# One order for all seven MLP steps, and the last block of the second MLP started on token tiles 0 and 1

## The chip, the cores and the metric

One core of a Trainium2 chip. The metric is the device time of one execution in microseconds (us), the median of several runs. A profile of one further execution shows what each engine did. The engines are TensorE (PE: matrix products; its weight loads are shown as PEld), VectorE (DVE), ScalarE (ACT), GpSimd (POOL) and SyncE (SP, which issues most transfers). Each engine takes the instructions of its own queue in the order in which the program holds them; semaphores make one engine wait for another.

## The reference

Four layers on 512 tokens of width 1024: a mixer with latent attention, an MLP, a mixer with gated linear attention, and a second MLP, each behind an RMS norm and added to the residual; a last RMS norm ends it. The change concerns the MLPs and the last norm alone:

```python
def sq_relu_mlp(xn, w_up, w_down):
    hid = jnp.square(jax.nn.relu(xn @ w_up))
    return hid @ w_down
...
        x = x + sq_relu_mlp(rms_norm(x, norm_mlp[i]), mlp_w_up[i], mlp_w_down[i]).astype(x.dtype)
    return rms_norm(x, final_norm)
```

`w_up` is 1024 x 4096 and `w_down` 4096 x 1024, all in float32.

## The kernel before, in words

**Precision.** A float32 operand is split into two parts of a faster type, high and low (`split`, L122): ACT copies it to the high part (L124), DVE subtracts that from the source to get the low part (L127). A product then takes three matmuls in place of one: high x high, high x low, low x high. `piece` does this for weights (buffers `wh` and `wl`, four of each, used in turn), `parts_of_quad` for a piece of hidden values (four pairs of buffers in turn; a pair with a negative sign is made by L870 and L871). A split writes its buffers only when the matmuls that read their old content are done.

**The MLP** (`mlp`). The 4096 hidden columns are taken in eight blocks of 512. The first block comes from `up_first`. Then seven steps, b = 0 to 6, each compute the hidden values of block b + 1 (up) and add block b's part to the result (down). Both are 2 x 2 block products with seven products instead of eight (Strassen's scheme in Winograd's form): the halves are the two halves of the tokens, of the model width and of the block's columns. The four hidden quads are q11, q12, q21, q22. The seven up-products are named 11, T1, T2, 21, T3, 22 and T4 (24 matmuls of 256 columns each, L993). The seven down-products are d11, d12, d11 + dS1 (here d11'), d12' , S21 (with d22), S5 (with dS1) and the one with dS3: 24 matmuls of 256 columns in the first MLP (MLP 0, L1006), 12 of 512 columns in the second (MLP 1, L1013). The sums of weights are made by transfers of POOL that add to what is in memory (S1, dS1, dS3, half of A2) and by DVE (a11 + S1 and so on).

Results are kept in `S11`, `S12`, `S21`, `SU` and `S5`. Some products go on from what others left in PSUM, so ACT copies a bank or a pair of banks before the next product changes it: product 11 to `y`, T1 to `w2`, and the two-bank sum `d` to `e` (L1021 in the first step, L1130 in the others). `finish` turns an up-product to hidden values: DVE's relu and scale (L885), ACT's square (L886).

PSUM has eight banks here: four single ones, tag "u", and two tiles of two banks each, "d" and "e". A two-bank tile used as two halves is still one tile to the program's tracking of dependencies.

**Two kinds of step.** Step b = 0 is `step` (L1016): up- and down-products alternate, and S5's sum starts fresh in a two-bank tile. Steps 1 to 6 are `step_in_halves` (L1123): seven up-products, then seven down-products. Weights are fetched for the next block as soon as a buffer is free (`after`).

**The last block of MLP 1** (L1270 to L1328). No up-products are left. The four token tiles t of 128 rows by two column halves c are eight row pieces, 12 matmuls of 512 columns each (L1303). A sum is copied into PSUM first by ACT, so the matmuls add to it. For c = 0, the sums of tiles 2, 3 lie in "e" (S12, L1272) and those of 0, 1 in "d" (S11, L1288); for c = 1 each piece has a single bank (L1294). The order is tiles 2, 3, 0, 1. Behind each piece follow the square and its sum along the row (ACT, L1306); for c = 0 a product with the gain (DVE, L1309), for c = 1 the norm's factor (L143, L1315 to L1317), the scaled output of this half (DVE, L1320, reads the PSUM sum) and of the other (ACT, L1322), and their transfers (L1321, L1323).

The order of instructions on each engine is the scheduler's of the framework: it mostly follows the order of the code, and takes an instruction later when its operands or buffers would not be there yet.

Of the kernel before, what the change touches and what calls it, by code (L numbers as in the profile page):

```python
# [15 lines left out]
ALU = mybir.AluOpType  # L16
# [34 lines left out]
def trunk_kernel(ctx: ExitStack, tc: tile.TileContext, t_in: dict, out: bass.AP):  # L51
# [778 lines left out]
    def mlp(layer, nrm, nxt=None):  # L830
# [185 lines left out]
        def step(b, q, r, after):  # L1016
            (q11, q12), (q21, q22) = q

            def begun(src):
                t = two_banks("e")  # L1020
                ACT.activation(t, src, AF.Copy)  # L1021
                return t

            def add(total, t):
                DVE.tensor_tensor(total, laid(t), total, ALU.add)

            def onto(tag, total, a, parts, fresh=False):
                t = two_banks(tag)
                if not fresh:
                    ACT.activation(laid(t), total, AF.Copy)  # L1030
                down_product(t, a, parts, fresh)
                ACT.activation(total, laid(t), AF.Copy)

            A1, A2, s1 = W["A1"], W["A2"], W["S1"]
            a11, a12, s3, a22 = A1[:, :KH], A1[:, KH:], A2[:, :KH], A2[:, KH:]
            d11, d12, ds1, ds3, d22 = (W[n] for n in ("d11", "d12", "dS1", "dS3", "d22"))

            z = bank("u")
            up_product(z, a11, "11", True)
            y = bank("u")  # L1040
            ACT.activation(y, z, AF.Copy)

            d = two_banks("d")
            down_product(d, d11, parts_of_quad(q11), True)
            e = begun(d)

            up_product(y, a12, "21", False)
            finish(y, 0, 0, r)
            DVE.tensor_tensor(a11, s1, a11, ALU.add)

            down_product(e, d12, parts_of_quad(q21), False)
            add(S11, e)
            DVE.tensor_tensor(d11, ds1, d11, ALU.add)
            DVE.tensor_tensor(q12, q22, q12, ALU.subtract)
            DVE.tensor_tensor(q11, q11, q12, ALU.add)

            part = {"e": e}

            def down_11():
                down_product(d, d11, parts_of_quad(q11, -1.0), False)  # L1060
                part["e"] = begun(d)
                DVE.tensor_tensor(d12, d11, d12, ALU.add)
                after("d11")

            def up_t2():
                up_product(z, a11, "T2", False)
                u = part["u"] = tmp()
                ACT.activation(u, z, AF.Copy)
                DVE.tensor_tensor(a12, a11, a12, ALU.add)

            def up_t1():
                w = part["w"] = bank("u")
                up_product(w, s1, "T1", True)
                w2 = part["w2"] = bank("u")
                ACT.activation(w2, w, AF.Copy)  # L1075
                after("S1")

            def down_22():
                e = part["e"]
                down_product(e, d12, parts_of_quad(q22), False)  # L1080
                add(S12, e)
                after("d12")

            def down_12():
                down_product(d, ds3, parts_of_quad(q12), False)
                add(SU, d)
                after("dS3")
                DVE.tensor_tensor(q22, q22, q11, ALU.subtract)

            def up_22():  # L1090
                w = part["w"]
                up_product(w, a12, "22", False)
                c = tmp()
                DVE.tensor_tensor(c, w, part["u"], ALU.add)
                finish(c, 0, 1, r)
                after("A1")

            def up_t3():
                up_product(z, s3, "T3", False)
                v = tmp()  # L1100
                ACT.activation(v, z, AF.Copy)  # L1101
                c = tmp()
                DVE.tensor_tensor(c, part["w2"], v, ALU.add)
                finish(c, 1, 1, r)

            def down_5():
                onto("e", S5, ds1, parts_of_quad(q22, -1.0), True)
                after("dS1")
                DVE.tensor_tensor(q21, q21, q11, ALU.subtract)

            def down_21():
                onto("d", S21, d22, parts_of_quad(q21, -1.0))
                after("d22")

            def up_t4():
                up_product(z, a22, "T4", False)
                finish(z, 1, 0, r)
                after("A2")

            for product in (up_t2, down_11, up_t1, down_22, up_22, up_t3, down_12, up_t4, down_5, down_21):  # L1120
                product()

        def step_in_halves(b, q, r, after):  # L1123
            (q11, q12), (q21, q22) = q
# [8 lines left out]
            def onto(total, a, parts):  # L1133
                pair = [bank("u"), bank("u")]
                cols = [part_of(total, i) for i in range(2)]
                for p, c in zip(pair, cols):
                    copied(laid(p), c)
                down_product(pair, a, parts, False)
                for p, c in zip(pair, cols):
                    copied(c, laid(p))  # L1140
# [45 lines left out]
            onto(S5, ds1, parts_of_quad(q22, -1.0))  # L1186
# [11 lines left out]
        for name in ("S1", "dS1", "d11", "A1", "d12", "dS3", "A2", "d22"):  # L1198
            fetch(0, name)
# [71 lines left out]
        loaded = {1: two_banks("e")}  # L1271
        ACT.activation(loaded[1], S12, AF.Copy)  # L1272
# [8 lines left out]
        rows = {}  # L1281
        for c in range(2):
            for th in (1, 0):
                total = (S11, S12, S21, SU)[2 * c + th]
                if c == 0:
                    if th not in loaded:
                        loaded[th] = two_banks("d")
                        ACT.activation(loaded[th], total, AF.Copy)  # L1288
                    o = loaded[th]
                for i in range(2):  # L1290
                    cs = slice(i * 512, (i + 1) * 512)
                    if c:
                        o = bank("u")
                        ACT.activation(o, total[:, cs], AF.Copy, scale=-1.0)  # L1294
                    rows[2 * th + i, c] = total[:, cs], o if c else o[:, cs]
# [588 lines left out]
```

## Time and profile before

| | |
|---|---|
| median of 3 runs | 1044.69 us (1044.43 to 1044.73) |
| profiled execution | 1042.52 us |
| its span, first to last instruction | 1040.8 us |
| mean granted TensorE clock | 0.999 |
| PE busy | 1030.6 us (99%) |
| DVE busy | 878.5 us (84%) |
| ACT busy | 695.1 us (67%) |
| POOL busy | 113.2 us (11%) |

How to read the lines shown below. The chain of waits goes back from the last instruction to what released each step; its lines give start, length, engine, tile and line, and "x24" the number of instructions. A line of the list of waits gives the waiting engine and line, the one it waited for, the total in us, the number of waits and the longest. A group of instructions shows the line, engine and operation, what is written and read, the shape, the count, then the busy time in us, the mean duration in ns, and the idle time before. A line of the timeline starts with the start and the busy time in us. A line of windows gives the window, its length, the busy time of PE, PEld, DVE, ACT and POOL (with the number of instructions), the granted clock, the share of the DMA engines and GB/s.

### The profile page before, as it was taken

How to read it: one execution, taken by the hardware profiler on the slowest of the kernel's cores; microseconds unless marked ns; L12 is line 12 of the kernel's file. 1: busy time of each engine (PE TensorE's matmuls, PEld its weight loads, DVE VectorE, ACT ScalarE, POOL GpSimd, SP SyncE). 2: the span in 40 equal slices, each digit the busy share in tenths (PEclk: the TensorE clock that was granted, in tenths of full speed). 3: DMA queues.
4: the chain of work that ended last, by engine and by line, in shares of the span. 5: the costliest groups of instructions: out<-in, count | busy, mean ns of one | idle time of the engine just before them, and what ended most of it. 6: DMA issues, size and time to landing. Idle time of an engine off the chain costs nothing.

```text
span 1040.8 us, 16839 instructions
## 1 busy us (share of the span) xinstructions
PE 1030.6 (99%) x6522; PEld 923.2 (89%) x6522; DVE 878.5 (84%) x1343; ACT 695.1 (67%) x1122; POOL 113.2 (11%) x128
## 2 busy tenths in 40 slices
PE   9999999999999999999999999999999999999997
PEld 8788888899999999998888888888889989989985
DVE  7889976899989989989686499469898899898993
ACT  7667754667776876785345565655677677677684
POOL 8400000401101111000000000000011101111000
PEclk9999999999999999999999999999999999999999
DMA  7401214759988778623313212164488777878422
GB/s 234 123 21 41 78 45 148 200 134 223 234 195 204 180 198 203 150 82 122 91 41 95 95 54 82 51 163 148 98 239 203 188 199 191 203 182 198 106 82 82
DMA packets 120001, 145.85 MB, mean 140 GB/s; under 512 B 9488, under 2 KB 86288, under 8 KB 119920
## 3 DMA queue, kind: packets, MB, share of 16 engines
q1 hardware_dynamic: 95424, 113.57, 34.2%
q0 software_dynamic: 22400, 29.36, 17.8%
q10 hardware_dynamic: 2096, 1.84, 0.6%
q8 instruction: 51, 0.84, 0.3%
q14 instruction: 30, 0.25, 0.1%
HBM read 142.39 MB, written 2.10 MB: 139 GB/s over the span
## 4 chain that ended last, share of the span: by engine, by line
PE 92%; DVE 4%; ACT 2%; DMA 1%; issue 1%; SPq 0%; ACTq 0%; DVEq 0%
PE ps L993 25%; PE ps L1006 12%; PE ps L1013 12%; PE ps L132 10%; PE ps L133 10%; PE ps L134 10%; PE ps L1303 2%; PE ps L1264 2%; PE ps L149 1%; PE ps L1523 1%; PE ps L436 1%; PE ps L1650 1%; DVE wl L127 1%; ACT wh L124 1%; DMA comb<-in_mlp_w_down_dram 1%
## 5 line engine op out<-in xcount | busy, mean ns | idle before, releaser
L124 ACT ACTIVATE wh<-wraw 128x1024 fp32r<-128x1024 f32 x139 | 146.3, 1056 | 108.6 <-issue 37.0
L127 DVE TENSOR_TENSOR wl<-wraw,wh 128x1024 fp32r<-128x1024 f32 x139 | 169.5, 1220 | 36.6 <-ACT wh L124 35.8
L993 PE MATMUL ps<-T,wh 128*128 128x256 f32 x896 | 154.8, 275 | 0.1
L127 DVE TENSOR_TENSOR wl<-comb,wh 128x1024 fp32r<-128x1024 f32 x112 | 136.7, 1221 | 16.7 <-ACT wh L124 16.5
L124 ACT ACTIVATE wh<-comb 128x1024 fp32r<-128x1024 f32 x112 | 118.5, 1058 | 47.8 <-issue 28.8
L993 PEld LDWEIGHTS ps<-T,wh 128*128 128x128 f32 x896 | 135.1, 188 | 0.5 <-ACT tmp L1101 0.3
L993 PE MATMUL ps<-T,wl 128*128 128x256 f32 x448 | 123.3, 275 | 0.0
L1013 PE MATMUL ps<-wh,set 128*128 128x512 f32 x392 | 122.8, 390 | 0.2 <-ACT set L124 0.2
L993 PE MATMUL ps<-set,wh 128*128 128x256 f32 x672 | 117.0, 276 | 0.3 <-ACT ps L1075 0.2
L132 PE MATMUL ps<-set,wh 128*128 128x512 f32 x280 | 109.6, 391 | 0.0
L133 PE MATMUL ps<-set,wh 128*128 128x512 f32 x280 | 109.5, 391 | 0.0
L134 PE MATMUL ps<-set,wl 128*128 128x512 f32 x280 | 109.2, 390 | 0.0
L1006 PE MATMUL ps<-hidden_parts,wh 128*128 128x256 f32 x784 | 106.6, 275 | 0.0
L993 PEld LDWEIGHTS ps<-set,wh 128*128 128x128 f32 x672 | 101.9, 188 | 1.4 <-ACT ps L1075 0.4
L1006 PEld LDWEIGHTS ps<-hidden_parts,wh 128*128 128x128 f32 x784 | 97.0, 188 | 0.0
L993 PE MATMUL ps<-set,wl 128*128 128x256 f32 x336 | 92.6, 276 | 0.0
L1013 PEld LDWEIGHTS ps<-wh,set 128*128 128x128 f32 x392 | 73.5, 188 | 15.3 <-ACT set L124 0.4
L993 PEld LDWEIGHTS ps<-T,wl 128*128 128x128 f32 x448 | 84.1, 188 | 0.0
L1013 PE MATMUL ps<-wl,set 128*128 128x512 f32 x196 | 76.3, 389 | 0.0
L993 PEld LDWEIGHTS ps<-set,wl 128*128 128x128 f32 x336 | 63.1, 188 | 0.0
L134 PEld LDWEIGHTS ps<-set,wl 128*128 128x128 f32 x280 | 52.6, 188 | 11.0
L133 PEld LDWEIGHTS ps<-set,wh 128*128 128x128 f32 x280 | 52.6, 188 | 10.9 <-DVE set L765 0.2
(426 smaller groups left out, 2209.8 us busy)
## 6 DMA issues: line engine op xcount, KB each, us to landing
comb<-in_mlp_w_down_dram SPq DMA_DIRECT2D x74, 512.0 KB, 4.4
wraw<-in_mlp_w_up_dram SPq DMA_DIRECT2D x18, 1024.0 KB, 5.6
wraw<-in_mlp_w_up_dram SPq DMA_DIRECT2D x28, 512.0 KB, 5.8
comb<-in_mlp_w_down_dram POOLq DMA_DIRECT2D x28, 512.0 KB, 6.8
wraw<-in_gla_w_in_dram SPq DMA_DIRECT2D x12, 1024.0 KB, 5.2
comb<-in_mlp_w_up_dram SPq DMA_DIRECT2D x14, 512.0 KB, 4.6
comb<-in_mlp_w_up_dram POOLq DMA_DIRECT2D x14, 512.0 KB, 7.3
wraw<-in_mlp_w_up_dram POOLq DMA_DIRECT2D x14, 512.0 KB, 7.6
```

The lines of the kernel that those rows point to most:

```text
L124: order(ACT.activation(hi, src, AF.Copy))
L127: lo_eng.tensor_tensor(lo, src, f(hi), ALU.subtract)
L132: PE.matmul(psum, wh, xh, start=start, stop=False)
L133: PE.matmul(psum, wh, xl, start=False, stop=False)
L134: PE.matmul(psum, wl, xh, start=False, stop=stop)
L149: PE.transpose(psum, src, ident[: src.shape[0], : src.shape[0]])
L436: PE.matmul(p, w[:, i, j * P : (j + 1) * P], x, start=start, stop=stop)
L993: PE.matmul(o, a_, x_, start=start and j == 0 and k == 0 and n == 0, stop=k == KH - 1 and n == 2, skip_group_check=True)
L1006: PE.matmul(o, w_[:, k, j * P : (j + 1) * P], x_[:, ts], start=opens, stop=k == 1 and n == 2, skip_group_check=True)
L1013: PE.matmul(o, x_, w_, start=start and k == 0 and n == 0, stop=k == 1 and n == 2, skip_group_check=True)
L1264: PE.matmul(p, a, x, start=k == 0 and n == 0, stop=k == 3 and n == 2)
L1303: PE.matmul(o, a, b_, start=False, stop=k == 3 and n == 2, skip_group_check=True)
```

## The change

`step` goes, and `step_in_halves` takes its name and is used for every b; in it `onto` gets a flag so that S5's first sum starts fresh. The names of the first fetches are put in another order. In the last block of MLP 1 the sums are seeded by one helper: tiles 0 and 1 in single banks for both column halves, tiles 2 and 3 in the halves of "e" (c = 0) and of "d" (c = 1), and the pieces are computed in the order 0, 1, 2, 3. The hidden quads are split in that order too. The number of matmuls stays the same.

```diff
-            def onto(total, a, parts):
+            def onto(total, a, parts, fresh=False):
                 pair = [bank("u"), bank("u")]
                 cols = [part_of(total, i) for i in range(2)]
-                for p, c in zip(pair, cols):
-                    copied(laid(p), c)
-                down_product(pair, a, parts, False)
+                if not fresh:
+                    for p, c in zip(pair, cols):
+                        copied(laid(p), c)
+                down_product(pair, a, parts, fresh)
...
-            onto(S5, ds1, parts_of_quad(q22, -1.0))
+            onto(S5, ds1, parts_of_quad(q22, -1.0), b == 0)
...
-        for name in ("S1", "dS1", "d11", "A1", "d12", "dS3", "A2", "d22"):
+        for name in ("A1", "S1", "A2", "d11", "dS1", "d22", "d12", "dS3"):
             fetch(0, name)
...
-            (step_in_halves if b else step)(b, Q[b % 2], Q[(b + 1) % 2], after)
+            step(b, Q[b % 2], Q[(b + 1) % 2], after)
...
+        rows = {}
+
+        def seed(o, total, th, c, sign=1.0):
+            for i in range(2):
+                cs = slice(i * 512, (i + 1) * 512)
+                rows[2 * th + i, c] = total[:, cs], o[i]
+                ACT.activation(o[i], total[:, cs], AF.Copy, scale=sign)
+
+        seed([bank("u"), bank("u")], S11, 0, 0)
-        for h, th in ((0, 0), (0, 1), (1, 1), (1, 0)):
+        for h, th in ((0, 0), (0, 1), (1, 0), (1, 1)):
             hid[h, th] = parts_of_quad(q[h][th])
+        seed(split_banks("e"), S12, 1, 0)
...
+        seed([bank("u"), bank("u")], S21, 0, 1, -1.0)
+        seed(split_banks("d"), SU, 1, 1, -1.0)
...
         for c in range(2):
-            for t in (2, 3, 0, 1):
+            for t in range(NT):
                 row(t, c)
```

In the code after the change `step` stands at L1016 to L1087 (its copies to PSUM and from it are L1023), the seeds at L1171, the matmuls of the last block at L1192, and the scaled output of a piece that reads its sum at L1209.

Where the program now holds its instructions, at the three places that matter. In the rows the tile written stands left of the arrow, those read right of it, with their buffer numbers, and in brackets whose semaphores the instruction waits for.

First, ACT's queue in MLP 1's first step. `set_1269` before and `set_1271` after is the first of the four buffers for high parts of hidden quads, and `set_1261` before and `set_1263` after is q11. Before, q11's high part stands among the squares of the first block (L902):

```order
L902 ACTIVATE set_1261_7838<-tmp_1291_7932 128x256 [waits DVE_49]
L902 ACTIVATE set_1262_7839<-tmp_1291_7932 128x256
L124 ACTIVATE wh_1327_8151<-wraw_1314_8086 128x1024 [waits PE_49]
L902 ACTIVATE set_1263_7840<-tmp_1299_7996 128x256 [waits DVE_49]
L902 ACTIVATE set_1264_7841<-tmp_1299_7996 128x256
L124 ACTIVATE set_1269_7846<-set_1261_7838 128x512 [waits Activation_49]
```

After, it stands behind the high part of the weights of d11' (`wh_1361`), whose buffer T4's weights had, and behind the squares of 22 and T4 (L886). The last two rows are a split into the same buffer, which waits for d11's matmuls, and the copy of `d` (`ps2_1350`) to `e` (`ps2_1353`):

```order
L124 ACTIVATE wh_1361_8409<-comb_1316_8092 128x1024 [waits PE_49,Activation_49]
L886 ACTIVATE set_1268_7848<-tmp_1344_8297 128x512 [waits DVE_49]
L886 ACTIVATE set_1269_7849<-tmp_1348_8330 128x512 [waits DVE_49]
L124 ACTIVATE set_1271_7851<-set_1263_7843 128x512
L124 ACTIVATE set_1273_7853<-set_1265_7845 128x512
L124 ACTIVATE set_1271_7851<-set_1266_7846 128x512 [waits DVE_49,PE_49]
L1023 ACTIVATE ps2_1353_8356<-ps2_1350_8337 128x1024 [waits PE_49]
```

The split of q11 has moved from the work of the first block to a place behind the last up-product's finish.

Second, PE's queue at the same place: d12's product on `e`. Before (`e` is `ps2_1326`, `d` is `ps2_1323`) it stands among the matmuls of an up-product:

```order
L993 MATMUL ps_1319_8099<-T_1306_8029,wl_1333_8206 128x256
L993 MATMUL ps_1319_8099<-T_1306_8029,wh_1332_8205 128x256
L1013 MATMUL ps2_1326_8149<-wh_1330_8185,set_1271_7848 128x512 [waits PE_49,Activation_49]
L1013 MATMUL ps2_1326_8149<-wl_1331_8186,set_1271_7848 128x512
L993 MATMUL ps_1319_8099<-T_1306_8029,wh_1332_8205 128x256
```

After, its first three matmuls stand right behind d11's twelve, ahead of S21's (`ps_1354`):

```order
L1013 MATMUL ps2_1350_8337<-wl_1352_8341,set_1271_7851 128x512
L1013 MATMUL ps2_1350_8337<-wh_1351_8340,set_1272_7852 128x512
L1013 MATMUL ps2_1353_8356<-wh_1359_8390,set_1273_7853 128x512 [waits Activation_49]
L1013 MATMUL ps2_1353_8356<-wl_1360_8391,set_1273_7853 128x512
L1013 MATMUL ps2_1353_8356<-wh_1359_8390,set_1274_7854 128x512 [waits DVE_49]
L1013 MATMUL ps_1354_8366<-wh_1356_8370,set_1275_7855 128x512 [waits PE_49,Activation_49]
```

The first matmul on `e` has moved from the middle of an up-product to the place directly behind the product that `e` is a copy of.

Third, PE's queue at the very end: the last two pieces. Before, each has a bank of its own (`ps_1707`, `ps_1708`), and a piece begins when ACT has seeded it:

```order
L1303 MATMUL ps_1707_10900<-set_137,set_1269_7846 128x512 x2
L1303 MATMUL ps_1707_10900<-set_137,set_1270_7847 128x512
L1303 MATMUL ps_1708_10902<-set_137,set_1271_7848 128x512 [waits Activation_49]
L1303 MATMUL ps_1708_10902<-set_137,set_1271_7848 128x512
L1303 MATMUL ps_1708_10902<-set_137,set_1272_7849 128x512
```

After, they are the halves of one tile (`ps2_1712`), and the second one's first matmul waits for DVE:

```order
L1192 MATMUL ps2_1712_10913<-set_137,set_1271_7851 128x512 x2
L1192 MATMUL ps2_1712_10913<-set_137,set_1272_7852 128x512
L1192 MATMUL ps2_1712_10913<-set_137,set_1275_7855 128x512 [waits DVE_49]
L1192 MATMUL ps2_1712_10913<-set_137,set_1275_7855 128x512
L1192 MATMUL ps2_1712_10913<-set_137,set_1276_7856 128x512
```

The wait is for the scaled output of tile 2 (L1209), the only one of DVE's instructions that reads this tile before.

More of the change, by code (lines that the diff above doesn't have):

```diff
@@ L1017, in step @@
             (q11, q12), (q21, q22) = q
[L1019 to L1121, printed above, removed]
@@ L1123, in step_in_halves @@
-        def step_in_halves(b, q, r, after):
-            (q11, q12), (q21, q22) = q
             A1, A2, s1 = W["A1"], W["A2"], W["S1"]
@@ L1270, in mlp @@
         hid = {}
-        loaded = {1: two_banks("e")}
-        ACT.activation(loaded[1], S12, AF.Copy)
-        for h, th in ((0, 0), (0, 1), (1, 1), (1, 0)):
+        rows = {}
[6 more added lines that the diff above has]
+        for h, th in ((0, 0), (0, 1), (1, 0), (1, 1)):
             hid[h, th] = parts_of_quad(q[h][th])
+        seed(split_banks("e"), S12, 1, 0)
         DVE.tensor_tensor(S21, S21, SU, ALU.add)
@@ L1280, in mlp @@
         stats = [sm(3) for _ in range(NT)]
[L1281 to L1295, printed above, removed]
+        seed([bank("u"), bank("u")], S21, 0, 1, -1.0)
+        seed(split_banks("d"), SU, 1, 1, -1.0)
         def row(t, c):
```

## The prediction

> **What bounds the kernel now.** I read the busy times first, then TensorE's waits, then the chain of waits through the three places that the change touches, and last the clock.
>
> ```profile
> PE 1030.6 (99%) x6522; PEld 923.2 (89%) x6522; DVE 878.5 (84%) x1343; ACT 695.1 (67%) x1122; POOL 113.2 (11%) x128
> ```
>
> TensorE (PE) is busy for 1030.6 of 1040.8 us. No other engine can set the time except by making PE wait, and the waits on PE are few:
>
> ```profile
> PE ps L1790 <- DVE ones L195: 1.2, 1, 1.2
> PE ps L1303 <- ACT ps L1272: 1.0, 1, 1.0
> ...
> PE ps L993 <- ACT ps L1075: 0.2, 1, 0.2
> PE ps L1013 <- ACT set L124: 0.2, 1, 0.2
> ```
>
> Three of the four lie where the change works: L1303 is the last block, L993 behind L1075 is the first step of MLP 0, L1013 behind L124 is the first step of MLP 1. Since the count of matmuls doesn't change, the forecast is a sum of PE waits removed and PE waits added. The later steps already have the order that the first one gets, and the chain shows what they cost:
>
> ```profile
> 245.91 19.04 PE ps L993 x168
> 264.95 19.04 PE ps L1006 x168
> ...
> 782.06 19.09 PE ps L993 x168
> 801.14 19.07 PE ps L1013 x84
> ```
>
> A settled step is nothing but PE: 38.08 us in MLP 0 and 38.16 us in MLP 1. From the same rows come the pitches: 19.09/168 = 0.114 us from one 256-column matmul to the next, 19.07/84 = 0.227 us for 512 columns, 2.73 us for one up-product (a seventh of 19.09) and 2.72 us for one down-product.
>
> **MLP 0, first step: a gain.** Before, this step runs from 206.35 to 245.91, and the next one is the settled step:
>
> ```profile
> 206.35:245.91 39.56, 39.16 (x339) 38.56 (x338) 38.97 (x45) 27.44 (x36) 5.34 (x5) 1.00 0.69 179
> 245.91:283.99 38.08, 38.08 (x338) 38.08 (x338) 35.27 (x39) 29.38 (x41) 5.00 (x4) 1.00 0.85 208
> 228.23 0.59 ACT ps L1075
> ...
> 236.90 0.49 ACT tmp L1101
> ```
>
> The first number after the window is its length, the next PE's busy time. The old step is 1.48 us longer than a settled one. Two of the pauses are the chain's detours over ACT's copies (L1075 of T1's bank, L1101 of T3's): the old order follows each copy too soon with a product that needs it. The settled order puts a whole product between a copy and its use, and takes both out. The copy of product 11 (now L1038) is still needed early, by 21, but T1 and T2 now stand between. The hidden quad q11 is split long before its use here, since ACT issues that split among the copies of the first block, as it did before. S1 is now used by the second product instead of the fifth, and POOL, which adds its second quadrant, issued that long ago:
>
> ```profile
> 183.28 1.45 POOL L982 DMA_DIRECT2D comb<-in_mlp_w_up_dram  x1 [103.62 <-DMA comb<-in_mlp_w_up_dram]
> 681.64 1.30 POOL L982 DMA_DIRECT2D comb<-in_mlp_w_up_dram  x1 [184.53 <-PE ps L149]
> ```
>
> That is 20 us and more ahead of the step here, and some 60 ahead in MLP 1. SP's issues keep their order up to the step. In the steps, transfers for the next block are issued in the settled order, in which PE's list has no wait for a DMA: cost nothing, cover over 20 us. I take -1.2 us of the 1.48, with -1.5 if all goes and -0.9 if the pause at the start stays.
>
> **MLP 1, first step: a loss.** Here the order of ACT's rows shows what the chain of before can't. Before, q11's high part was made early, 9 us ahead of the first down-product:
>
> ```profile
> 735.67 0.73 ACT L902 ACTIVATE set<-tmp 128x256 f32<-128x256 f32 x2 [0.86 <-DVE tmp L900]
> 736.31 0.62 ACT L124 ACTIVATE set<-set 128x512 fp32r<-128x512 f32 x1
> ...
> 748.43 0.63 ACT L124 ACTIVATE set<-set 128x512 fp32r<-128x512 f32 x1 [1.10 <-PE ps L1013]
> 748.97 1.01 ACT L1021 ACTIVATE ps<-ps 128x1024 f32<-128x1024 f32 x1
> 749.91 1.04 ACT L124 ACTIVATE wh<-comb 128x1024 fp32r<-128x1024 f32 x1
> ...
> 745.87 2.54 PE ps L1013 x11
> ```
>
> From the start of that down-product to the next step are 36.19 us (745.87 to 782.06), with six up-products and seven down-products: 6 x 2.73 + 7 x 2.72 = 35.4. So this step loses 0.8 us, which the new order takes away (-0.8).
>
> After the change the first down-product comes behind all seven up-products, and q11's split stands on ACT's queue behind everything that it issues up to the finish of T4: first the high part of d11's second weights (it reuses the buffer of T4's weights, so it waits for T4's matmuls), then two squares (L886), and only then q11. ACT and DVE take their rows in order. The durations:
>
> ```profile
> L124 ACT ACTIVATE wh<-comb 128x1024 fp32r<-128x1024 f32 x112 | 118.5, 1058 | 47.8 <-issue 28.8 <-PE ps L993 9.5 <-PE ps L133 2.5
> L886 ACT ACTIVATE set<-tmp 128x512 f32<-128x512 f32 x56 | 33.4, 616 | 4.7 <-DVE tmp L885 4.7
> L124 ACT ACTIVATE set<-set 128x512 fp32r<-128x512 f32 x34 | 21.4, 629 | 15.0 <-PE ps L1013 13.5 <-DVE set L416 1.5
> L885 DVE SCALAR_TENSOR_TENSOR tmp<-ps,rstd 128x512 f32<-128x512 f32 x28 | 19.2, 686 | 5.5 <-PE ps L993 5.5
> L1182 DVE TENSOR_TENSOR comb<-comb,comb 128x1024 f32<-128x1024 f32 x12 | 14.6, 1213 | 0.0
> L127 DVE TENSOR_TENSOR wl<-comb,wh 128x1024 fp32r<-128x1024 f32 x112 | 136.7, 1221 | 16.7 <-ACT wh L124 16.5
> L127 DVE TENSOR_TENSOR set<-set,set 128x512 fp32r<-128x512 f32 x34 | 23.6, 696 | 1.8 <-ACT set L124 1.7
> ```
>
> ACT can begin on the weights about 0.1 us after PE would be due with the down-product; then 1.06 + 0.62 + 0.62 + 0.63 = 2.93, less three overlaps of 0.07 to 0.09 between rows that follow each other (735.67 + 0.73 reaches past 736.31, 748.97 + 1.01 past 749.91), so 2.7, and a hop of 0.04 to PE (as from 1010.93 + 1.04 to 1012.01, below): the high part comes 2.8 us late. DVE has the finish of T4, the add d12 += d11, the low part of the weights and then q11's low part: 0.2 + 0.69 + 1.21 + 1.22 + 0.70, less 0.24 of overlap, so 3.8 us after the due time. It is read by the third matmul, at 2.8 + 2 x 0.227 = 3.3: another 0.5. First new wait: 3.4 us (2.8 to 3.8).
>
> The second is behind d11's product. PE's next three matmuls are those of d12's product, which write the "e" copy of what d11 has just made, and on ACT a hidden quad's split stands between. Before, the same pair of ACT rows (748.43 and 748.97) followed the eleventh matmul's end at 748.41 (745.87 + 2.54) and ended at 749.98. PE would be due again at 745.87 + 12 x 0.227 = 748.59, so the wait is 749.98 + 0.04 - 748.59 = 1.4 us. Before, an up-product was there to fill that time; now none is. In the settled steps the three matmuls don't stand there, and S21's product fills it. Further down I allow 0.3 us (0 to 0.8) for a low part behind DVE's adds. The sum: 3.4 + 1.4 + 0.3 - 0.8 = +4.3 us (3.2 to 5.2).
>
> **The last block: a gain at its start, a larger loss at its end.**
>
> ```profile
> 1000.64 1.22 DVE L1179 TENSOR_TENSOR xT<-ps,xT 128x1024 f32<-128x1024 f32 x1
> ...
> 1009.76 1.15 DVE xT L1189
> 1010.93 1.04 ACT ps L1272
> 1012.01 22.32 PE ps L1303 x96
> ...
> 1033.70 0.61 PE L1303 MATMUL ps<-set,set 128*128 128x512 f32 x2
> ...
> 1036.09 0.75 DVE L1320 SCALAR_TENSOR_TENSOR xT<-ps,sm,comb 128x512 f32<-128x512 f32 x1
> 1036.84 0.37 ACTq L1323 DMA_DIRECT2D out_dram<-xT  x1
> ```
>
> Before, the block's first tile is tile 2, whose sum S12 is the last but one to be finished: DVE's add, ACT's copy into two banks, then PE, with a wait of 1.0 in the list above. A 512-column matmul is 390 ns long at a pitch of 227, so over the pitch it is 1.0 + 0.16 = 1.16 us. Tile 0's sum S11 is added some nine us earlier and copied into its banks ahead of the last steps' work, so this wait goes: -1.2 us.
>
> At the other end the last two tiles now lie in the two halves of one two-bank tile, and tile 3's first matmul waits for DVE's last row of tile 2 (the scaling of its output, L1320 before, L1209 now), as the order shows. That chain is quoted for before's last tile. The last two matmuls start at 1033.70 and 0.227 later, so a further one would be due at 1034.15; L1320 ends at 1036.84. With the hop of 0.04 the wait is 1036.88 - 1034.15 = 2.7 us, and PE stands first of its queue with twelve matmuls behind it. Before, the four sums of this half were single banks, and there was no such wait. In the first half the same sharing exists before and after, at no more than this, since other tiles' matmuls are put between:
>
> ```profile
> PEld ps L1303 <- DVE xT L1309: 0.3, 1, 0.3
> ```
>
> The tail nets 2.7 - 1.2 = +1.5 us (1.2 to 1.9).
>
> The Trainium skill, PSUM — Partial Sum Buffer, section "The four PSUM rules", says that each bank is a separate physical SRAM. By that the chip would not need the wait, and the tail would be -1.2; the wait of 0.3 in the row above, on the same kind of pair, speaks for the program's wait being obeyed.
>
> **Sum.** -1.2 + 4.3 + 1.5 = +4.6 us on the profiled execution's 1042.52, of which the span is 1040.8: 1047.1, span 1045.4. The median of the runs, 1044.69, lies 2.2 us above the profiled execution; I carry the difference over: 1044.69 + 4.6 = 1049.3 us.
>
> **The rivals.**
>
> *The late splits cost nothing* (other side: not slower). ACT's place in the printed order is not a time. If ACT ran so far ahead that q11's split were done when PE reaches d11, and the "e" copy too, the 5.1 us would be gone: -1.2 - 0.8 + 1.5 = -0.5, 1044.2 us. For it: ACT is busy 67% of the span. Against it: ACT's row ahead of the split waits for T4's matmuls, and the square of T4 can't begin before T4 ends and DVE has taken 0.69 us for its finish; 0.2 + 0.69 + 0.62 + 0.63 = 2.1 us remain even if the weights cost nothing. It decides at the moment T4's last matmul starts: q11 must be on its way by then. Chance 0.06.
>
> *The tail's wait is not there*, or covered. Then -1.2 + 4.3 - 1.2 = +1.9: 1046.6 us. For it: only tile 3's own bank is written while tile 2's is read. Against: the wait stands in the order, and its like is in the trace. Chance 0.08.
>
> *The clock falls in the new pauses.* PE has never been idle for over 1.2 us inside this kernel, but it is after its last matmul (1034.31), and the granted clock follows (seventh number behind each window's busy times, 0.96 and 0.50):
>
> ```profile
> 1037.00:1038.00 1.00, 0.00 (x0) 0.00 (x0) 0.00 (x0) 0.00 (x0) 0.00 (x0) 0.96 0.29 111
> 1038.00:1039.00 1.00, 0.00 (x0) 0.00 (x0) 0.00 (x0) 0.00 (x0) 0.00 (x0) 0.50 1.04 389
> ```
>
> With 0.96 as the mean of a slice at 1 and 0.5, it fell at 1037.9, 3.6 us after PE stopped. My pauses are 2.8 (with two matmuls before the next 0.5) and 2.7, both shorter. If the fall came earlier, half speed for as long again as it took, 3.6 us, would cost 1.8 us at each place: 1049.3 + 3.6 = 1052.9 us. Chance 0.08.
>
> The Trainium skill, TensorE: Matmul & The Clock Gate, section "What's actually happening", says that the clock is halved after at least one idle window of some 3.4 us, and that these windows run free of the kernel. By that rule a pause of 2.8 us fills no window and the sum stays at +4.6; the fall after 3.6 us agrees with it.
>
> **How the numbers follow.** My forecast, both waits about as priced, has 0.74, the rivals 0.06, 0.08 and 0.08, and 0.04 is left for what I haven't seen. The forecast's own bounds: the low ends -1.5 + 3.2 + 1.2 = +2.9, 1047.6; the high ends -0.9 + 5.2 + 1.9 = +6.2, 1050.9. The range reaches down to the case without the tail's wait, 1046.5, and up to 1051.0; it leaves out the first rival and the clock's. A change of under 0.2%, 2.1 us, can't be told from none here, so "same" is 1042.6 to 1046.8: the first rival and the second, of which a part lies above, and some of the rest, 0.12. Faster needs more gains than I found, 0.02. Slower: 0.86.
>
> **What would show it.** In the changed kernel's list of PE's waits: L1013 behind ACT's L124 with about 2.8 us and behind DVE's L127 with 0.5; L1013 behind ACT's L1023 with over 1 us; L1192 behind DVE's L1209 with 2.5; none behind L1171 at the start of the last block. In the chain, MLP 0's first step should be near 38.3 us, and MLP 1's second step should begin 3.1 us later than 782.06 (-1.2 + 4.3). Wrong would be a first down-product in MLP 1 that follows T4 without a pause, a tile 3 that starts right behind tile 2, or a granted clock under 1 between 740 and 1035 us.

## The result: 0.49% slower

| | before | after |
|---|---|---|
| median of 4 runs | 1044.65 us (1044.43 to 1044.73) | 1049.57 us (1048.8 to 1050.81) |
| profiled execution | 1042.52 us | 1049.03 us |
| its span | 1040.8 us | 1047.3 us |
| mean granted TensorE clock | 0.999 | 0.997 |
| PE busy | 1030.6 us (99%) | 1031.1 us (98%) |

The ratio is 1.0049, 95% interval 1.0031 to 1.0066. Two repeats on other chips gave 1.0067 (1.0049 to 1.0085) and 1.0066 (1.0054 to 1.0078). The medians above lie 4.9 us apart; from 1044.65, the three ratios put the change at +5.1, +7.0 and +6.9 us; +4.6 had been forecast. One of the six runs of the first repeat took 2685.89 us at a granted clock of 1.0 and isn't in its ratio; no trace shows why. The runs of the changed kernel lie 2 us apart in the first measurement, where the four of before lay 0.3 apart; in the later ones, with 21 to 28 runs each, those of before lie 3.3 to 5.5 us apart.

### The profile page after: what moved, and what is told of

Same layout as the page of the kernel before. It is cut to its first block, busy times and chain, and to the rows that moved or that the text cites. A ratio compares the mean times of both kernels' runs of the same rounds, so it can differ in the third digit from the quotient of the medians.

```text
span 1047.3 us, 16859 instructions
## 1 busy us (share of the span) xinstructions
PE 1031.1 (98%) x6522; PEld 922.9 (88%) x6522; DVE 879.3 (84%) x1343; ACT 696.2 (66%) x1130; POOL 112.7 (11%) x128
## 4 chain that ended last, share of the span: by engine, by line
PE 90%; DVE 4%; ACT 3%; DMA 2%; issue 1%; SPq 0%; ACTq 0%; DVEq 0%
PE ps L993 25%; PE ps L1013 13%; PE ps L1006 13%; PE ps L132 10%; PE ps L134 10%; PE ps L133 10%; PE ps L1158 2%; PE ps L1192 2%; PE ps L1412 1%; PE ps L149 1%; DVE wl L127 1%; DMA wraw<-in_mla_w_in_dram 1%; PE ps L1539 1%; ACT wh L124 0%; DVE acc L266 0%
## 5 line engine op out<-in xcount | busy, mean ns | idle before, releaser
L1013 PE MATMUL ps<-wh,set 128*128 128x512 f32 x392 | 123.5, 393 | 4.2 <-ACT set L124 2.7
L1013 PEld LDWEIGHTS ps<-wh,set 128*128 128x128 f32 x392 | 74.0, 189 | 20.7 <-ACT set L124 2.8
L1013 PE MATMUL ps<-wl,set 128*128 128x512 f32 x196 | 76.8, 392 | 0.0
```

Of the source, the lines that this page charges most:

```text
L1013: PE.matmul(o, x_, w_, start=start and k == 0 and n == 0, stop=k == 1 and n == 2, skip_group_check=True)
```

## The profile after

The list of PE's waits of the changed kernel has the three lines that were forecast, and at nearly their sizes (2.8, "over 1" and 2.5 had been named), and the fourth with 0.2 instead of 0.5:

```profile
PE ps L1192 <- DVE xT L1209: 3.0, 1, 3.0
PE ps L1013 <- ACT set L124: 2.7, 1, 2.7
PE ps L1013 <- ACT ps L1023: 1.4, 1, 1.4
...
PE ps L1013 <- DVE set L127: 0.2, 1, 0.2
```

The waits on L1075 and at the start of the last block (L1272 before) are gone. The chain of waits through the same places, with start and length:

```profile
244.57 19.04 PE ps L993 x168
...
764.94 3.34 PE ps L1013 x9
768.30 0.63 ACT set L124
768.93 0.92 ACT ps L1023
769.89 16.67 PE ps L1013 x72
786.56 19.09 PE ps L993 x168
...
1036.98 0.76 DVE xT L1209
1037.78 3.07 PE ps L1192 x12
...
1042.61 0.75 DVE xT L1209
```

And the first matmul of MLP 0's first step and of the last block, from the timeline:

```profile
206.10 0.40 PE L993 MATMUL ps<-set,wh 128*128 128x256 f32 x2
...
1015.36 0.62 PE L1192 MATMUL ps<-set,set 128*128 128x512 f32 x2
```

These starts cut the kernel into four stages, which can be compared without the shifts that one hands to the next. The starts of before are 206.35, 245.91, 782.06 and 1012.01 (quoted with the prediction), and its span ends at 1040.81, that of the changed kernel at 1047.33.

| stage, in us | before | after | change | forecast |
|---|---|---|---|---|
| 1: MLP 0's first step (206.10 to 244.57) | 39.56 | 38.47 | -1.1 | -1.2 |
| 2: from there to MLP 1's second step (to 786.56) | 536.15 | 541.99 | +5.8 | +4.3 |
| 3: from there to the last block (to 1015.36) | 229.95 | 228.80 | -1.15 | -1.2 |
| 4: the last block, to the end of the span (1047.33) | 28.8 | 32.0 | +3.2 | +2.7 |

In each stage the sign of the change is as forecast, and every wait is where it was put. Between the two profiled executions the sum is +6.5, though (what lies ahead of stage 1 came out 0.25 shorter), and not +4.6: the terms of stages 2 and 4 are too small.

What stage 2 holds beyond the forecast shows in PE's timeline around the first pause (its last up-product's matmul, then d11's), in three rows of DVE, and in the windows over the same time:

```profile
760.66 0.28 PE L993 MATMUL ps<-T,wl 128*128 128x256 f32 x1
763.59 0.76 PE L1013 MATMUL ps<-wh,set 128*128 128x512 f32 x1 [2.65 <-ACT set L124]
764.15 0.63 PE L1013 MATMUL ps<-wl,set 128*128 128x512 f32 x1
764.94 1.22 PE L1013 MATMUL ps<-wh,set 128*128 128x512 f32 x2 [0.16 <-DVE set L127]
```

```profile
760.73 0.69 DVE L885 SCALAR_TENSOR_TENSOR tmp<-tmp,rstd 128x512 f32<-128x512 f32 x1
761.33 0.68 DVE L885 SCALAR_TENSOR_TENSOR tmp<-ps,rstd 128x512 f32<-128x512 f32 x1
...
764.20 0.69 DVE L127 TENSOR_TENSOR set<-set,set 128x512 fp32r<-128x512 f32 x1
```

```profile
763.00:764.00 1.00, 0.41 (x1) 0.41 (x2) 1.00 (x2) 1.00 (x3) 0.00 (x0) 0.83 1.21 195
764.00:767.00 3.00, 2.84 (x7) 1.74 (x7) 2.97 (x6) 0.06 (x1) 0.00 (x0) 0.50 0.69 195
767.00:768.00 1.00, 1.00 (x6) 0.82 (x5) 0.42 (x1) 0.00 (x0) 0.00 (x0) 0.96 0.14 53
```

The pause is 763.59 - 760.66 - 0.11 = 2.8 us, as forecast. The third matmul, due 0.454 after the first, comes 0.9 late instead of 0.5: DVE begins T4's finish at 761.33, not at T4's end, since it was still at the finish of product 22 (the row at 760.73). PE's list counts only 0.16 of this, since the two matmuls ahead already ran at a lower clock and ended later. And the granted clock, third number from the end of a window's line, is 0.5 from 763.7 (0.83 is the mean of a slice at 1 and 0.5) to 767.1, for 3.4 us. The last block's pause is longer by ACT's own transfer:

```profile
1034.81 0.38 ACTq L1212
1035.24 0.70 ACT tmp L1195 x2
```

Tile 2's square waits for ACT to issue tile 1's output; before, the program held the last square ahead of that issue.

## The experiments

All were timed in five rounds beside the kernel before, whose median was 1043.39, 1043.16 and 1043.72 us on the three chips. The theory: the loss is q11's and q21's late splits and the shared two-bank tile, each with a clock that falls. The stages of the profiled executions, in us:

| kernel | 1 | 2 | 3 | 4 | ratio to before (95%) |
|---|---|---|---|---|---|
| before | 39.56 | 536.15 | 229.95 | 28.8 | 1 |
| after | 38.47 | 541.99 | 228.80 | 32.0 | 1.0049 (1.0031 to 1.0066) |
| after, 2nd | 38.57 | 542.86 | 228.80 | 33.5 | 1.0067 (1.0049 to 1.0085) |
| after, 3rd | 38.47 | 542.43 | 228.79 | 33.3 | 1.0066 (1.0054 to 1.0078) |
| early q11 and q21, both MLPs | 39.85 | 536.29 | 228.79 | 34.4 | 1.0026 (1.0016 to 1.0036) |
| early q11, MLP 1 | 38.39 | 537.09 | 228.80 | 33.5 | 1.0018 (1.0009 to 1.0026) |
| single banks | 38.37 | 542.44 | 228.79 | 28.7 | 1.0024 (1.0016 to 1.0033) |
| early, both MLPs, and single banks | 39.90 | 536.35 | 228.79 | 28.7 | 0.9982 (0.9973 to 0.999) |
| early, MLP 1, and single banks | 38.41 | 536.18 | 228.80 | 29.0 | 0.997 (0.9961 to 0.9979) |
| pauses filled | 38.34 | 540.94 | 228.79 | 31.9 | 1.0044 (1.0031 to 1.0057) |
| pauses filled, 2nd | 38.42 | 540.88 | 228.80 | 31.9 | 1.004 (1.0028 to 1.0052) |
| last block alone | 41.31 | 536.16 | 228.80 | 33.5 | 1.0033 (1.0022 to 1.0044) |
| MLP 0's step alone | 38.43 | 536.16 | 229.96 | 28.8 | 0.9979 (0.997 to 0.9987) |
| d11 and dS1 exchanged | 38.89 | 540.80 | 229.22 | 28.8 | 1.0021 (1.0009 to 1.0034) |

### Early splits of q11 and q21

```diff
+            p11 = parts_of_quad(q11) if b == 0 else None
+            p21 = parts_of_quad(q21) if b == 0 else None
             w, w2, z, y = (bank("u") for _ in range(4))
...
-            down_product(d, d11, parts_of_quad(q11), True)
+            down_product(d, d11, p11 or parts_of_quad(q11), True)
...
-            p21 = parts_of_quad(q21)
+            p21 = p21 or parts_of_quad(q21)
```

> The changed kernel, but in the first step of both MLPs the splits of q11 and q21 are written ahead of the up-products instead of ahead of d11 and d12. Late splits (mine): both waits of MLP 1's first step go, which the changed kernel's trace puts at 2.8 + 0.9 us for q11's parts, 1.6 us for the copy to e, and 1.1 us of matmuls at half clock behind the first; PE's list has no wait of L1013 on L124 or L1023 over 0.4 us, the tail keeps its 3.0; about -6 us, 1043.5. Rival, d11's weights or their transfer come late: the split's place doesn't matter, the pause after T4 stays over 2 us and the time within 1 us of the changed kernel's 1049.6.

Measured: 1046.18 us, ratio 1.0026, so 2.4 to 4.3 us less than the changed kernel's three ratios, not 6. Stage 2 did what was expected: from 541.99 to 536.29, with no wait of L1013 left in PE's list. Two things hid it. In MLP 0 the earlier splits pushed other rows of ACT and DVE back, so that PE now waits for a copy (L1023): stage 1 is 39.85 instead of 38.47. And the last block's wait is the same 3.0 us, but the clock fell in it:

```profile
PE ps L1194 <- DVE xT L1211: 3.0, 1, 3.0
...
PE ps L993 <- ACT tmp L1023: 0.9, 1, 0.9
```

```profile
1033.59 5.50 PE ps L1194 x12
```

```profile
1032.00:1033.00 1.00, 0.00 (x0) 0.00 (x0) 0.60 (x3) 0.49 (x3) 0.00 (x0) 0.89 0.91 338
...
1039.00:1040.00 1.00, 0.07 (x1) 0.00 (x0) 0.16 (x1) 0.86 (x3) 0.00 (x0) 0.70 0.00 0
```

Tile 3's twelve matmuls take 5.50 us here and 3.07 in the first trace of the changed kernel. By the means of the slices the clock fell at 1032.8, while PE still waited, and came back at 1039.6, 6.8 us later. The late splits are shown as the cause of stage 2's loss; the rival (d11's weights) falls, since those weights were left as they were.

### Early split of q11 alone, in MLP 1

```diff
+            p11 = parts_of_quad(q11) if b == 0 and not nxt else None
...
-            down_product(d, d11, parts_of_quad(q11), True)
+            down_product(d, d11, p11 or parts_of_quad(q11), True)
```

> The changed kernel, with q11's split alone written early, in MLP 1's first step alone. The first wait there goes (2.8 and 0.9, and its share of the clock), the wait of d12 for the copy to e stays at 1.4 to 1.6 since S21's product still isn't ready, the tail keeps its 3.0: 4 to 5 us less than the changed kernel, and the clock falls only at the end. Rival, the two waits have one cause: the second goes too (6 us less), or none does.

Measured: 1045.43 us against the changed kernel's 1050.48 on the same chip, 5.1 less. Its list of PE's waits:

```profile
PE ps L1193 <- DVE xT L1210: 3.0, 1, 3.0
PE ps L1013 <- ACT ps L1023: 1.4, 1, 1.4
```

The first wait is gone, the copy's wait stays: two separate causes, the late split of q11 and that of q21. Stage 2 is 537.09, that is 0.9 more than with q21 early as well. With q21's split early too, the program puts S21's product behind d11's, and the copy to `e` is hidden.

### Single banks for the last two pieces

```diff
-        seed(split_banks("d"), SU, 1, 1, -1.0)
+        seed([bank("u"), bank("u")], SU, 1, 1, -1.0)
```

> The changed kernel, with one edit: the sums of tiles 2 and 3 for the second column half are seeded in two single banks instead of the halves of one two-bank tile. Shared tile (mine): the wait of 3.0 us behind DVE's scaled output goes, -2.9 us, 1046.7; the first step of MLP 1 keeps its waits of 2.7 and 1.4. Rival, the end is set by the rows of ACT and DVE, of which a tile needs 2.9 us and PE only 2.7: then PE ends 3 us earlier and the last tile's chain starts late, and less than half is gained, 1048.3 or more.

Measured: 1046.1 us, ratio 1.0024, against 1.0049 and more for the changed kernel. Stage 4 falls from 32.0 to 28.7 and PE's list has no wait for DVE's output left. The end of the chain:

```profile
1035.88 0.70 ACT tmp L1195 x2
...
1038.24 0.68 ACT tmp L1195 x2
...
1039.95 0.75 DVE xT L1209
```

Tile 3's square comes 2.36 us behind tile 2's, not 2.9: here the program holds it ahead of the issue of tile 2's transfer. ACT doesn't set the end, so that rival falls. The stage on which the edit acts shows the loss whole: it came with the one tile that held both banks.

### Both edits, and the version that beats both kernels

The two edits above in one kernel, first with the splits early in both MLPs:

> Both edits in one kernel: early splits of q11 and q21, and single banks for the last two pieces. Mine: the gains add, about -9 us on the changed kernel, 1040.5; against the kernel before what is left is the gain in MLP 0 (1.3), the 0.8 of MLP 1's first step and about 1.1 at the start of the last block, so 1041 to 1042 and below before. Rival, the gains of the one order are taken back by something else that the pauses covered (transfers for the next block, ACT's backlog): near the kernel before, 1044 to 1045.

Measured: 1041.43 us, ratio 0.9982, so below before by 0.18%. Expected were 1040.5 by one reckoning and 1041 to 1042 by the other; the second holds. Its stage 1 is again long (39.90). So then the early splits in MLP 1 alone:

```diff
+            p11 = parts_of_quad(q11) if b == 0 and not nxt else None
+            p21 = parts_of_quad(q21) if b == 0 and not nxt else None
...
-        seed(split_banks("d"), SU, 1, 1, -1.0)
+        seed([bank("u"), bank("u")], SU, 1, 1, -1.0)
```

> The changed kernel with q11's and q21's splits early in MLP 1's first step alone (MLP 0's as in the changed kernel) and single banks for the last two pieces. The earlier kernel with both edits had the early splits in MLP 0 too, where its first step came out 1.5 us longer than in the changed kernel. So 1.5 us less than that one: about 3.5 us less than the kernel before, 0.34%. Rival, that 1.5 us was chance: 2 us less than the kernel before, as the earlier one.

Measured: 1040.21 us, ratio 0.997, 3.1 us less than before, near the 3.5 expected, and 1.2 us less than the one before it (measured on another chip), though the two intervals overlap a little. Its chain, at MLP 1's second step and at the last block:

```profile
780.65 19.09 PE ps L993 x168
...
1009.61 13.89 PE ps L1194 x60
```

Stage 2 is 536.18, as before the change. The 0.8 us that the old first step of MLP 1 loses aren't won: with the early splits in it, the new order costs as much. In the chain of this trace two detours stand in the step, one over ACT's copy L945, which comes behind q21's split (739.50), and one over DVE's L871 (764.18); they weren't taken out by a run. Of the 3.1 us, MLP 0's first step alone makes 2.2, as a run below shows.

### The pauses filled with useless matmuls

In the cut, `spend` is 24 for d11 in MLP 1's first step and 0 elsewhere.

```diff
+            for _ in range(spend):
+                PE.matmul(t[:, :256], wh[:, 0, :P], quad["11"][0][:, 0], start=True, stop=True, skip_group_check=True)
...
+                if (t, c) == (3, 1):
+                    o = bank("u")
+                    for _ in range(11):
+                        PE.matmul(o, hid[0, 1][0][:, :P], last[1][0][0], start=True, stop=True, skip_group_check=True)
```

> The changed kernel with useless matmuls in its two long pauses: 24 of 256 columns into d ahead of d11's product in MLP 1's first step (2.7 us, overwritten by the product's first matmuls), and 11 of 512 columns into a free single bank between tiles 2 and 3 at the end (2.5 us). No wait is taken away. Clock (mine): the granted clock stays at 1 through both places, about -1.1 us in the median, 1048.4, and the runs lie within 0.5 us of each other. Rival, the clock costs nothing and the spread is something else: 1049.6 or slower by up to 0.5, with runs 2 us apart as in the changed kernel.

> The kernel with useless matmuls in the two long pauses again, beside the changed kernel on one chip. The granted clock at 0.999 in nearly all runs, runs within 1.5 us of each other; 1.5 to 3 us less than the changed kernel although it does more. Rival, the clock costs nothing: within 0.5 us of the changed kernel.

> The changed kernel, beside these on one chip: 5 to 7 us more than the kernel before, granted clock 0.994 to 0.998 and the time the longer the lower the clock.

Measured: 1047.62 us the first time (runs 1047.27 to 1048.56), 1047.68 the second (1047.41 to 1048.21), the latter beside 1050.48 (1048.78 to 1051.14) for the changed kernel on the same chip: 2.8 us less with 35 matmuls more. The first time, the ratio of 1.0044 (1.0031 to 1.0057) can't be told from the changed kernel's first 1.0049, and its runs lie 1.3 us apart, not 0.5; it is the second, beside the changed kernel, that parts them. The clock was 0.998 or 0.999 in all ten of these runs and 0.995 in four of the changed kernel's five there; its fifth, at 0.997, was its shortest. From the chain of the second filled kernel, its d11 and its tile 3, and the windows around both pauses:

```profile
764.89 2.35 PE ps L1015 x9
...
1036.74 3.03 PE ps L1194 x12
```

```profile
755.00:770.00 15.00, 12.99 (x94) 11.61 (x93) 14.07 (x19) 9.49 (x14) 1.28 (x1) 1.00 0.64 157
1030.00:1041.00 11.00, 9.30 (x40) 7.05 (x38) 3.57 (x11) 5.67 (x15) 0.00 (x0) 1.00 0.39 144
```

The same nine matmuls take 2.35 us here and 3.34 in the changed kernel's first trace: a fall costs 1.0 us there. The delays behind ACT and DVE stay, with the useless matmuls in them: stage 4 is 31.9, as in the trace without a fall there. The clock's part is shown. It is also part of why the changed kernel's runs spread, since its traces hold a fall in one place or in both; a run at 0.998 (1047.32 us, in the first repeat) may hold none, but no such run was traced, and before's own spread of 3.3 to 5.5 us is in it too.

### The changed kernel again

> The changed kernel itself, for its ratio beside the parts on one chip and for a second trace. The pauses are as before: 2.8, 0.9 and 1.6 us in MLP 1's first step, 3.1 at the end. If the clock falls where a pause meets it by chance, this trace may show it at another of the two places or at both, and the runs lie 2 us apart or more; if the spread is something else, the granted clock falls at the same place as in the first trace. Time +4.5 to +5.5 us on the kernel before.

Measured: ratio 1.0067, +7.0 us. Its trace has both falls, the clock 0.994. In MLP 1 the clock is down from 762.8 to 769.7, for 6.8 us, and the nine matmuls take 4.22 us. At the end the fall comes when PE is already back at work:

```profile
764.42 4.22 PE ps L1013 x9
...
1038.17 4.57 PE ps L1192 x12
```

```profile
1039.00:1040.00 1.00, 1.00 (x5) 0.77 (x4) 0.00 (x0) 0.00 (x0) 0.00 (x0) 0.65 1.02 385
1040.00:1042.00 2.00, 2.00 (x6) 1.63 (x5) 0.00 (x0) 0.00 (x0) 0.00 (x0) 0.50 0.18 64
1042.00:1043.00 1.00, 0.73 (x2) 0.01 (x1) 0.00 (x0) 0.23 (x1) 0.00 (x0) 0.64 0.00 0
```

By the means of the slices it falls at 1039.3, 1.1 us after the pause has ended at 1038.17, and returns at 1042.7, 3.4 us later; the twelve matmuls take 1.5 us more than the 3.07 of the first trace.

### The last block alone, and MLP 0's first step alone

The kernel before, with the last block of the changed kernel:

```diff
-            for t in (2, 3, 0, 1):
+            for t in range(NT):
```

and the seeds that belong to it, as in the diff of the change.

> The kernel before, with only the last block of MLP 1 as changed (seeds, order of tiles); both first steps as before. By the changed kernel's trace: the start 1.0 us earlier, the wait for tile 2's scaled output 3.1, so +2.1 us on the kernel before, and up to 1.5 more in the runs in which the clock falls in the last pause. Rival, the tail's loss hangs on the rest of the change (an earlier end of the steps): within 0.5 us of the kernel before.

Measured: 1046.35 us, ratio 1.0033, +3.4 us: the block costs the same without the rest of the change. Stage 3 gains 1.15, stage 4 loses 4.7 with a fall of the clock in it, where +2.1 and up to 1.5 more had been expected for the block. The other part alone, the new step in MLP 0:

```diff
-            (step_in_halves if b else step)(b, Q[b % 2], Q[(b + 1) % 2], after)
+            (step_in_halves if b or nxt else step)(b, Q[b % 2], Q[(b + 1) % 2], after)
```

with `onto`'s flag, and the new order of first fetches in MLP 0.

> The kernel before, with only MLP 0's first step in the one order (and its first fetches); MLP 1's first step and the last block as before. -1.3 us on the kernel before, the first step 38.3 us long instead of 39.6. Rival, what the step gains is lost again later in MLP 0: no change.

Measured: 1040.77 us, ratio 0.9979, -2.2 us; expected were -1.3. Its runs lie 1.7 us apart, those of before 5.5 on that chip. A likely reason shows when two traces with the old step are put side by side, the one before and the one with the last block alone. First PE's wait in the latter, then the windows of the old step there and of the new one in the kernel just named, then ACT's row for d11's weights, of the two with the old step:

```profile
PE ps L993 <- ACT ps L1041: 1.5, 1, 1.5
```

```profile
206.26:247.57 41.31, 39.46 (x339) 38.67 (x338) 39.15 (x45) 28.91 (x41) 6.19 (x5) 1.00 0.65 170
```

```profile
206.23:244.50 38.27, 38.27 (x339) 38.20 (x338) 38.10 (x44) 29.85 (x42) 5.75 (x5) 1.00 0.78 194
```

```profile
203.42 1.07 ACT L124 ACTIVATE wh<-comb 128x1024 fp32r<-128x1024 f32 x1 [3.98 <-DMA comb<-in_mlp_w_down_dram]
```

```profile
201.73 1.07 ACT L124 ACTIVATE wh<-comb 128x1024 fp32r<-128x1024 f32 x1 [2.40 <-DMA comb<-in_mlp_w_down_dram]
```

In the old step ACT stands idle until d11's transfer has landed, with the first block's squares and the copy to `y` behind it. When it lands 1.7 us later, PE waits 1.5 us for that copy. In the new step S1's weights are at this place on ACT's queue, which have long landed: stage 1 is 38.3 to 38.6 us in all the traces of it in which ACT's queue is as in the changed kernel.

### d11's transfer made early

```diff
-        home = {"S1": 0, "dS1": 1, "d11": 4, "d12": 3, "dS3": 2, "d22": 5}
+        home = {"S1": 0, "dS1": 4, "d11": 1, "d12": 3, "dS3": 2, "d22": 5}
```

> The kernel before, with the buffers of d11 and dS1 exchanged, so that d11's first transfer in MLP 0 doesn't wait for the end of the normalisation's last sums and lands some 10 us earlier; ACT's order is unchanged. In the two traces that hold the old first step of MLP 0, ACT stands idle until that transfer has landed (at 201.7 and at 203.4), with the copy to y behind it on its queue, and the step ends 1.7 us apart. If that is the cause of the spread of the kernel before: the idle time goes, the runs lie within 1.2 us, and the time is 1.5 to 2.5 us less than the kernel before. Rival, the spread has another cause: no change in the median, runs over 2 us apart.

Measured: 1045.76 us, ratio 1.0021, slower, with runs 5.4 us apart: a miss. The edit did in MLP 0 what it should. There is no wait for the transfer, and stage 1 is 38.89:

```profile
199.16 1.05 ACT L124 ACTIVATE wh<-comb 128x1024 fp32r<-128x1024 f32 x1
```

But it acts in MLP 1 too, where dS1's sum is now the late transfer. DVE waits for it, the first block's last rows stand behind it, and PE waits 3.0 us, with a fall of the clock behind it (744.3 to 747.7):

```profile
PE ps L941 <- ACT xT L945: 3.0, 1, 3.0
```

```profile
725.95 11.15 DMA comb<-in_mlp_w_down_dram
...
737.20 1.23 DVE comb L1053
```

So the traces show how d11's landing makes the old first step longer, but how much of the spread of before it makes was not isolated. The exchange in MLP 0 alone was not tried.

## Why the prediction was right, and where it wasn't

The direction and the measured time were right, the waits at each place too. That the time came out within 0.3 us was luck: between the profiled executions the sum was 1.9 us too small (+6.5, not +4.6), and of the 2.2 us that the prediction carried over from profile to median the changed kernel had only 0.5 in the first measurement. In the two repeats, where the ratios give +7.0 and +6.9, nothing made up for the missing terms. And one of the three things that the prediction named as a sign of being wrong did come, a granted clock under 1 between 740 and 1035 us.

- **MLP 0, first step** (-1.2): -1.1 between the profiled executions, and -2.2 in the medians of the run with this step alone. No wait for the earlier uses of S1 and the other weights came up. What failed is the step "I carry the difference over": 2.2 us between profile and median became 0.5. In the profiled execution of before, d11's weights were taken up at 201.7 and not at 203.4 as in the other trace with the old step, and the new step doesn't hang on that transfer. That this makes up the missing 1.7 us is argued, not shown, since the exchange that should have shown it missed.
- **MLP 1, first step** (+4.3): +5.8. The second step begins 4.5 us later than before (786.56 against 782.06), where 3.1 had been named. The pause behind T4 is 2.8 us as priced, the copy's wait 1.4 in PE's list as priced. The low part's wait was mis-sized (0.5, measured 0.9: DVE had two finishes to do, not one), and the clock added 1.0. The 0.3 further down the step wasn't there as a wait. With the 0.8 taken off, 2.8 + 0.9 + 1.0 + 1.4 leave 5.3 of the 5.8; the rest wasn't traced to a wait.
- **The last block** (+1.5): +2.0 without a fall of the clock, +3.5 with one (in the second trace). The start is -1.15 against -1.2; the wait for tile 2's output 3.1 over the pitch against 2.7, by the issue of tile 1's transfer that ACT now does first.
- **The rivals.** Late splits that cost nothing, and a tail without its wait, fell. The clock was given 0.08 because both pauses were "shorter" than the 3.6 us it took to fall at the end of before. That step failed: it fell behind the pause of 2.8 us in the first trace and in both places in the traces of the two repeats. It isn't a rival to the sum but a part of it in most runs.

Of the Trainium skill's TensorE: Matmul & The Clock Gate, section "What's actually happening", the prediction drew that a pause under one window of some 3.4 us leaves the clock alone. Here the measurement decides against that. The length of a window in the Trainium skill agrees with the 3.4 us from most falls to the return; that its windows run free of the kernel fits a fall that comes 1.1 us behind the pause's end. Of the Trainium skill's PSUM — Partial Sum Buffer, section "The four PSUM rules", the prediction drew that each bank is a memory of its own: with a tile for each of the two banks the wait was gone, as separate memories would allow; whether the chip would have let PE write the one half of a shared tile while DVE reads the other was not tried.

## What to carry to other kernels

An order that is right for a settled loop needs its operands' first preparation to move with it: the first step's splits stood where the old step's first use was, and the scheduler put them behind everything written earlier. Where PE is at 99%, look on the other engines' queues at what stands ahead of the instruction that PE will wait for, transfer issues included. And one profiled execution can lie well below its median: before costs are carried over, look for a wait on a transfer that the median may hold longer.

## What the runs showed of the hardware

The granted clock fell to half at ten of the eleven pauses of PE of 2.8 to 3.1 us that the traces hold without useless matmuls in them; the eleventh is the end of the changed kernel's first trace. It didn't fall at the copy's wait of 1.4 us in MLP 1 where that stood without the longer pause (early split of q11 alone). The falls came from 0.8 us before PE resumed (1032.8 against 1033.59, early splits in both MLPs) to 1.4 us after (764.9 against 763.57, single banks). Eight of the ten lasted 3.4 us (763.7 to 767.1 and 1039.3 to 1042.7 are two of them), the other two 6.8 us (762.8 to 769.7 in the second trace of the changed kernel, 1032.8 to 1039.6 with the early splits). A fall cost 1.0 to 1.9 us of a product of 2.7 us in MLP 1 (its nine matmuls took 3.34, 3.84 and 4.22 us in the changed kernel's three traces, and 2.35 with the pause filled), and 1.3 to 2.4 us at the end. Useless matmuls in the pauses kept the clock at full there and made the kernel 2.8 us faster on one chip.
